# One encoder layer on one core: a fourteenth projection pair as seven half products, and the last gate tiles moved between the branch tiles

## Chip, core and metric

The kernel runs on one core of a Trainium2 chip. The metric is the device time of one execution in microseconds. Before the change three runs took 723.83, 724.24 and 725.03 us, so the median is 724.24 us.

## What is computed

One post-norm encoder layer in float32 on 512 tokens of width 1024, cut here to what matters:

```python
proj = h @ w_in[l]                       # q, k, v of both token mixers, 3840 columns
qa, ka, va, qb, kb, vb = jnp.split(proj, SPLITS, axis=-1)
o_a = windowed_gqa_sink(qa, ka, va, a_sink[l])     # 16 heads
o_b = dilated_mixture(qb, kb, vb)                  # 3 groups of 4 heads, merged
gates = jax.nn.sigmoid(h @ w_gate[l] + b_gate[l])  # 2048 columns
g_a, g_b = jnp.split(gates, N_BRANCH, axis=-1)
mixed = g_a * (o_a @ w_br_a[l]) + g_b * (o_b @ w_br_b[l])
y = mixed @ w_out[l]
h = layer_norm(DN_ALPHA * h + y, ln1_g[l], ln1_b[l])
f = (jax.nn.silu(h @ w_ff_gate[l]) * (h @ w_ff_up[l])) @ w_ff_down[l]
h = layer_norm(DN_ALPHA * h + f, ln2_g[l], ln2_b[l])
```

## The kernel before, in words

**Products.** A float32 product is made of three matmuls on rounded operands: every operand is split into a high part h (a copy rounded to fp32r, line 387 on ACT or 389 on DVE) and a low part l (the rest, a DVE subtraction, line 413 or 558), and h·h + h·l + l·h is added up in PSUM. A projection has units of 128 output columns: U_QA, U_KA, U_VA for mixer A, U_QKB, U_V0, U_VB for mixer B, and 16 gate tiles U_GATE. A unit alone (`feat_x`, lines 537 to 539) is 8 k-steps of three matmuls of 128x512, so 24, from four weight tiles (two h, two l) that `unit` loads and splits.

**Pairs.** `pair_x` (line 608) computes two units together by a seven-product scheme for 2x2 blocks: seven half products of 4 k-steps by three matmuls of 128x256 (lines 659 to 661), so 84 matmuls. It loads five blocks of weights by SP and adds two of them up by accumulating DMAs from POOL (line 401), forms S2 and S4 by two DVE additions (with the letter D: by DMA), splits seven operands, moves four halves out of PSUM by ACT (line 667), and adds the parts on DVE (lines 558 and 682). The combinations of x that it needs are formed once, by `x_forms`. Thirteen pairs are computed so; sixteen units are computed alone.

**Order.** Nothing is written out in queue order by hand. Each operation is given to `Program.op` with its engines, buffers and a priority; `Program.run` (line 207) goes through a model of the five engines in time and lets each free engine take the ready operation with the lowest priority whose buffers fit (`fits`, line 188). What comes out is a fixed instruction order for each engine. A priority is `pr.T` (the PE work given so far, in us) plus an offset: weights -130 (`LOOK`), evacuations -100 (`EV`). Buffers are counted in classes: 85 slots of 128x512, of which `gen`, `ws` (loaded weights) and `whl` (split weights) take shares; four `x4` buffers, which hold the split x until the last product that reads it; eight PSUM banks, of which at most three are of the class `dense` (`BANKS`), which all projections and branches use.

**ORDER** (line 87) is a string of words that `step` (line 1393) takes in turn: `q2` or `k1` a unit alone, `P:` or `D:` a pair, `g` a gate tile, `R` and `r` the rotary turn of the tiles that wait for it (`turn_rows`; r also by DMA), `A0` to `A3` and `B0` to `B3` an attention group, `O` the fetch of a tile of mixer A's output, `V0`, `V12`, `VA` values. `@-31` shifts the priority of that word by -31 us. Before the first word, five units run along each other while x arrives: k0, q0, the first value unit and two gate tiles; k0 and q0 are turned and split right behind that (`k_near`, `q_near`), which empties their PSUM banks.

**Branches.** After the last word come the 16 branch tiles in the order BRANCHES: `branch_a` (8 k-steps, from the fetched output of mixer A) and `branch_b` (2 k-steps), each multiplied by its gate tile (line 1482). `fetch_oa` (line 1365) fetches and splits mixer A's output; the high parts of tiles 4 to 7 (`N_XA` = 4) go into an `x4` buffer, so they wait for one that x has left. Gate tiles 8 to 15 are stored to DRAM and fetched again. Then come the output projection with the first layer norm (`tok_major`), 22 tiles of the channel mixer and the second norm.

Of the kernel before, what the change touches and what calls it, by code (L numbers as in the profile page):

```python
# [15 lines left out]
P = 128  # L16
S = 512
D = 1024
# [13 lines left out]
U_KA = 0  # L32
# [19 lines left out]
BIAS = 0.2  # L52
SPARE, SPARE2 = (4, 12)
ROOMS = {2: dict(whl=16), 3: dict(whl=20, ws=8)}
# [49 lines left out]

BRANCHES = "a0 a1 a2 a3 a4 b0 a5 b1 b2 a6 b3 b4 a7 b5 b6 b7"

# [31 lines left out]
class Program:  # L138


    def __init__(self, limits):
        self.limits = limits
        self.used = {k: 0 for k in limits}
        self.ops = []
        self.writer, self.readers = {}, {}
        self.T = 0.0
        self.spare = SPARE
        self.strict = self.hold = False
        self.rooms = {}

# [56 lines left out]
    def run(self):  # L207
# [27 lines left out]
        while n_left:  # L235
# [13 lines left out]
            while progress:  # L249
                progress = False  # L250
                for e in engines:
# [19 lines left out]
                    for b in o.bufs:  # L271
                        if b.tile is None:
                            if b.keys[0] in self.rooms:
                                b.room = self.rooms[b.keys[0]].popleft()
# [70 lines left out]
def hybrid_layer(ctx: ExitStack, tc: tile.TileContext, wpack, xT, xtok, sink, bgate,  # L345
# [111 lines left out]
    def unit(u):  # L457
        return [half_unit(u, 0), half_unit(u, 1)]
# [33 lines left out]
    for j in range(2):  # L492
        for w, u in (("k", U_KA), ("q", U_QA), ("v", U_VA), *((i, U_GATE + 8 + i) for i in range(N_ALONG))):
            first[w, j] = half_unit_by(u, j, ((0, S),) if j else ALONG_CUTS if w in range(N_ALONG) else CUTS, FIRST[w, j])
# [263 lines left out]

    def in_sbuf(u):

        ps, t = bank("dense"), slot()
        feat_x(ps, unit(u))
        op([(ACT, act(S, True))], lambda e: copy(ACT, halves(t.t), back(ps.t)), reads=[ps], writes=[(t, 1), (t, 2)], prio=EV)
        return t
# [518 lines left out]
    def gate_of(f, t):  # L1283
        gz[f] = t
        op([(ACT, act(S, False, 1))], lambda e: nc.scalar.activation(
            t.t, t.t, AF.Tanh, bias=bg.t[:, f:f + 1], scale=0.5), reads=[(t, 1), (t, 2), bg], writes=[t], prio=EV)
        if f in AWAY:
            put_away(f)
# [6 lines left out]
    def gate(f, ps=None):  # L1295
        if ps is None:
# [6 lines left out]
           reads=[ps, bg], writes=[t], prio=EV)  # L1303
        if f in AWAY:
            put_away(f)
# [6 lines left out]
    def dense_k(u, nt):  # L1312
        ps = bank("dense")
        feat_x(ps, unit(u))
        return k_post(ps, nt) if nt else k_pairs(ps)

    psk, psq, psv = bank("dense"), bank("dense"), bank("dense")
    along = [bank("s") for _ in range(N_ALONG)]
# [11 lines left out]
    for f in range(N_ALONG):  # L1330
        gate(8 + f, ps=along[f])
    ka, qa = {0: k_near(psk, 4)}, {0: q_near(psq, 4, (0, 0))}
    load(mB, maskb, prio=0)
    env = {"gate": N_ALONG, "turn": [], "qs": {}, "ks": {}}

# [29 lines left out]
    def fetch_oa(k):  # L1365
# [8 lines left out]
        return split_of(st, [st], OA_SPLIT, h=Part(xa[k // 4], k % 4) if k >= N_XA else None, by_blocks=True)  # L1374

    def units_of(w):
        i = int(w[1:] or 0)
# [9 lines left out]
        if w[0] == "k":  # L1387
            return U_KA + i, lambda t: ka.update({i: k_post(t, 4)})
        f = (env["gate"] + 8) % 16
        env["gate"] += 1  # L1390
        return U_GATE + f, lambda t: gate_of(f, t)

    def step(w):
        if w == "X":
            x_forms()
        elif w == "L":
            op([(POOL, 0.0)], lambda e: pr.limits.update(ws=N_WS, whl=N_WHL), after=[env["mark"]])
# [31 lines left out]
        elif w[0] in "gG":  # L1429
            for _ in range(int(w[1:] or 1)):  # L1430
                gate((env["gate"] + 8) % 16)
                env["gate"] += 1
        elif w[0] in "QK":
# [16 lines left out]

    for w in ORDER.split():
        w, _, later = w.partition("@")
        pr.T += float(later or 0)
        step(w)
        pr.T -= float(later or 0)
# [5 lines left out]
    op([(POOL, 0.0)], free_all, after=lasts)  # L1461


# [12 lines left out]

    sa.extend(fetch_oa(k) for k in range(len(sa), 8))
    MA = moving(sa)
    sm, sb_ = {}, []

# [13 lines left out]
    def branch_b(f):  # L1494
        if not sb_:
            sb_.extend(split_of(t, [(t, 0), (t, 1)], OB_SPLIT) for t in obT)
        if f % 4 == 0:
            env["wu"] = unit(U_BRB + f // 4)
        MB = moving(sb_)
        ps = bank("dense")  # L1500
        for k in range(2):
            feat_k(ps, env["wu"], k, MB, lambda k: [sb_[k][0].tok, sb_[k][1]], nk=2, col=lambda k: (k, (f % 4) * P))
        mark = gated(8 + f, ps)
# [4 lines left out]

    names = BRANCHES.split()
    marks = []  # L1510
    for n, w in enumerate(names):
        k = 8 + int(w[1])
        if w[0] == "b":
            if k in away:
                fetch_gate(k, [*exps, marks[names.index("b%d" % (k - 11))]] if k > 10 else exps)
        marks.append((branch_a if w[0] == "a" else branch_b)(int(w[1])))
    for w, mark in zip(names, marks):
        env[w] = [mark]


# [594 lines left out]
```

## Time and profile before

| | |
|---|---|
| median of three runs | 724.24 us |
| the profiled execution | 724.82 us |
| its span, first to last instruction | 723.0 us |
| PE busy | 712.5 us (99%), 4947 matmuls |
| DVE busy | 664.4 us (92%) |
| ACT busy | 494.6 us (68%) |
| POOL busy | 173.2 us (24%) |
| DMA | 141.44 MB, mean 196 GB/s |

The profiled execution has 1.8 us outside its span. A matmul's own duration (0.275 us for 128x256, about 0.38 us for 128x512) overlaps the next one; what it costs in a stream is the distance between two starts, which the timeline shows.

### The profile page before, as it was taken

How to read it: one execution, taken by the hardware profiler on the slowest of the kernel's cores; microseconds unless marked ns; L12 is line 12 of the kernel's file. 1: busy time of each engine (PE TensorE's matmuls, PEld its weight loads, DVE VectorE, ACT ScalarE, POOL GpSimd, SP SyncE). 2: the span in 40 equal slices, each digit the busy share in tenths (PEclk: the TensorE clock that was granted, in tenths of full speed). 3: DMA queues.
4: the chain of work that ended last, by engine and by line, in shares of the span. 5: the costliest groups of instructions: out<-in, count | busy, mean ns of one | idle time of the engine just before them, and what ended most of it. 6: DMA issues, size and time to landing. Idle time of an engine off the chain costs nothing.

```text
span 723.0 us, 14810 instructions
## 1 busy us (share of the span) xinstructions
PE 712.5 (99%) x4947; PEld 667.2 (92%) x4947; DVE 664.4 (92%) x1425; ACT 494.6 (68%) x1136; POOL 173.2 (24%) x347
## 2 busy tenths in 40 slices
PE   8999999999999999999999999999999999999996
PEld 6889999998999998988888999999999999999985
DVE  6998999999999989999958998999999999999987
ACT  5768889889878997767625666756567566666821
POOL 0113343322423591550020022121121201212000
PEclk9999999999999999999999999999999999999999
DMA  8978967887568789766690499776897868979402
GB/s 257 294 215 210 235 168 213 227 216 179 137 169 204 187 255 253 219 196 219 199 210 33 110 300 232 177 203 165 238 238 197 223 164 219 253 196 194 106 29 88
DMA packets 81275, 141.44 MB, mean 196 GB/s; under 512 B 11024, under 2 KB 15760, under 8 KB 81200
## 3 DMA queue, kind: packets, MB, share of 16 engines
q1 hardware_dynamic: 63472, 107.07, 46.3%
q0 software_dynamic: 17456, 33.30, 26.6%
q8 instruction: 39, 0.64, 0.4%
q14 instruction: 36, 0.29, 0.1%
q10 hardware_dynamic: 272, 0.13, 0.1%
HBM read 119.69 MB, written 8.39 MB: 177 GB/s over the span
## 4 chain that ended last, share of the span: by engine, by line
PE 90%; DMA 4%; DVE 3%; SPq 2%; ACT 1%; issue 0%; POOL 0%; DVEq 0%; ACTq 0%; POOLq 0%
PE ps L1761 10%; PE ps L1759 10%; PE ps L1760 9%; PE ps L659 5%; PE ps L661 5%; PE ps L660 5%; PE ps L537 4%; PE ps L538 4%; PE ps L539 4%; PE ps L1970 4%; PE ps L1972 4%; PE ps L1971 4%; PE ps L1018 3%; DMA sl<-wpack 3%; PE ps L1549 3%; PE ps L1551 3%
## 5 line engine op out<-in xcount | busy, mean ns | idle before, releaser
L387 ACT ACTIVATE sl<-sl 128x512 fp32r<-128x512 f32 (+3 forms) x457 | 253.8, 588 | 60.7 <-DVE sl L558 43.3
L558 DVE TENSOR_TENSOR sl<-sl,sl 128x512 fp32r<-128x512 f32 (+3 forms) x415 | 245.3, 628 | 6.0 <-ACT sl L387 5.0
L387 ACT ACTIVATE sl<-ps 128x256 f32<-128x256 f32 (+6 forms) x214 | 88.5, 440 | 76.6 <-PE ps L1761 53.0
L401 POOL DMA_DIRECT2D sl<-wpack x70 | 63.0, 931 | 319.1 <-DMA sl<-wpack 92.0
L1760 PE MATMUL ps<-sl,sl 128*128 128x256 f32 x352 | 96.8, 275 | 0.0
L1761 PE MATMUL ps<-sl,sl 128*128 128x256 f32 x352 | 96.8, 275 | 0.0
L1759 PE MATMUL ps<-sl,sl 128*128 128x256 f32 x352 | 96.8, 275 | 0.0
L1759 PE MATMUL ps<-x,sl 128*128 128x256 f32 x264 | 72.6, 275 | 0.0
L1760 PE MATMUL ps<-x,sl 128*128 128x256 f32 x264 | 72.6, 275 | 0.0
L1761 PE MATMUL ps<-x,sl 128*128 128x256 f32 x264 | 72.6, 275 | 0.0
L1759 PEld LDWEIGHTS ps<-sl,sl 128*128 128x128 f32 x352 | 67.6, 192 | 0.1
L1760 PEld LDWEIGHTS ps<-sl,sl 128*128 128x128 f32 x352 | 67.6, 192 | 0.1
L1761 PEld LDWEIGHTS ps<-sl,sl 128*128 128x128 f32 x352 | 67.6, 192 | 0.0
L537 PE MATMUL ps<-x,sl 128*128 128x512 f32 (+1 forms) x161 | 62.1, 386 | 0.7 <-ACT x L387 0.7
L539 PE MATMUL ps<-x,sl 128*128 128x512 f32 (+1 forms) x161 | 60.9, 378 | 0.0
L659 PE MATMUL ps<-sl,sl 128*128 128x256 f32 x208 | 57.8, 278 | 0.9 <-ACT sl L667 0.9
L661 PE MATMUL ps<-sl,sl 128*128 128x256 f32 x208 | 57.3, 276 | 0.0
L660 PE MATMUL ps<-sl,sl 128*128 128x256 f32 x208 | 57.2, 275 | 0.0
L558 DVE TENSOR_TENSOR sl<-sl,ps 128x512 f32<-128x512 f32 (+1 forms) x72 | 47.3, 661 | 9.0 <-PE ps L1972 5.8
L1759 PEld LDWEIGHTS ps<-x,sl 128*128 128x128 f32 x264 | 50.6, 192 | 0.4
L1760 PEld LDWEIGHTS ps<-x,sl 128*128 128x128 f32 x264 | 50.6, 192 | 0.4
L1761 PEld LDWEIGHTS ps<-x,sl 128*128 128x128 f32 x264 | 50.7, 192 | 0.0
(174 smaller groups left out, 2006.6 us busy)
## 6 DMA issues: line engine op xcount, KB each, us to landing
sl<-wpack SPq DMA_DIRECT2D x254, 256.0 KB
sl<-wpack POOLq DMA_DIRECT2D x70, 256.0 KB, 5.5
wf<-wpack SPq DMA_DIRECT2D x51, 256.0 KB
sl<-sl SPq DMA_DIRECT2D x56, 128.0 KB
wf<-wpack POOLq DMA_DIRECT2D x24, 256.0 KB, 5.3
oa<-sl POOLq DMA_DIRECT2D x32, 128.0 KB, 3.6
sl<-sl SPq DMA_DIRECT2D x72, 32.0 KB
gz<-sl SPq DMA_DIRECT2D x8, 256.0 KB
```

The costliest lines, as they stand in the source:

```text
L387: nc.scalar.activation(dst, src, AF.Copy)
L401: op([(POOL, 1.0)], lambda e: nc.gpsimd.dma_start(b.t, src2, accum_op=ALU.add), reads=[b], writes=[b], prio=prio, moves=1.65)
L537: mm(o, a, x0, start=(k == 0 and begins), stop=False, skip_group_check=split)
L538: mm(o, a, x1, start=False, stop=False, skip_group_check=split)
L539: mm(o, b, x0, start=False, stop=(k == nk - 1), skip_group_check=split)
L558: op([(DVE, dve(w))], lambda e: nc.vector.tensor_tensor(dst(), x(), y(), op=o), reads=reads, writes=writes, prio=prio)
L659: mm(o, wh, pairs(bh[k]()), start=(first and k == 0), stop=False, skip_group_check=True)
L660: mm(o, wh, pairs(bl[k]()), start=False, stop=False, skip_group_check=True)
L661: mm(o, wl, pairs(bh[k]()), start=False, stop=(k == 3), skip_group_check=True)
L1759: mm(o, wh, pairs(bh[k]()), start=(first and k == 0), stop=False, skip_group_check=True)
L1760: mm(o, wh, pairs(bl[k]()), start=False, stop=False, skip_group_check=True)
L1761: mm(o, wl, pairs(bh[k]()), start=False, stop=(k == 3), skip_group_check=True)
```

## The change

ORDER, its offsets and some constants are new. The number of words `P:` and `D:` goes from 13 to 14: two gate tiles that were `g` words (tiles 0 and 1) become one pair. k0 and q0 become words of ORDER (`first_of`), so their turning and splitting, and with it the emptying of their PSUM banks, comes at the place and priority of the word. The branch tiles become words of ORDER too; the word `/` runs `late()`, which frees the buffers of the attention and completes the fetches of mixer A's output. The last three gate tiles are 5, as a single unit, and 6 with 7, as a pair; they come behind `/`, just ahead of the branch words. Before, 5 and 6 were a pair, 7 was a single unit, and no branch tile had been given yet. `N_XA` = 8 puts the high parts of all eight tiles of mixer A's output into ordinary slots, none into an `x4` buffer. One turn word (that of Q02 and K02) goes from R to r. A PSUM bank for the accumulators `d` is preferably one that a whole-bank user held last (`room_for`).

```diff
-SPARE, SPARE2 = (4, 12)
+SPARE, SPARE2 = (6, 12)
...
 ORDER = """
-X@-11 VA@-23 q2@-799 q1@-877 P:q3,g@-124 R@-106 D:k1,q4@-31 R@155 P:q5,Q01@-843 A0@-168 D:q6,q7@-47 D:g,g@-34 r@631 P:g,Q00@-22 L@-4 A2@-96
-D:g,K00@-31 A1@-48 R@187 V12@-20 P:g,K01@-67 R@-5 P:Q02,K02@-28 A3@-55 V0@55 R@5 B0@-7 B1@11 O@25 O@35 P:K10,Q10@-39 O@-13 O@-54 K11@-34 R@24
-O@11 P:Q12,Q11@-30 g@28 K12@-12 O@950 g@25 r O@43 P:g,g@-2 B2@-525 O@-304 B3@21 g@-29 P:g,g@-32 g@-8
+X@8 q1@-832 q0@288 P:q3,g@-368 R@-92 D:k1,q4@-30 R@191 P:q5,Q01@-788 q2@-435 k0@40 VA@-106 A0@-163 D:q6,q7@-68 r@1450 D:g,g@-56 P:g,Q00@-1
+L@-33 A1@-75 D:g,K00@-2 A2@-90 V12@-10 R@-8 P:g,K01@-72 R@1 P:Q02,K02@-21 V0@23 r@-570 B0@-107 O@-104 A3@-82 O@-32 P:K10,Q10@-29 B1@-44 O
+K11@-15 O@40 R@696 O@-49 O@42 P:Q12,Q11@-7 P:g,g@13 K12@-34 O@-15 P:g,g@-31 r@-7 B2@-653 O@66 g@2 B3@-265 /@-12 g@21 P:g,g@-51 a0@14 a4@5
+b0@18 a1@-36 b1@7 a5@-3 a6@28 a3@-28 a2@-31 b3@6 b2@20 b4@46 a7@-19 b7@-26 b6@322 b5@-17
 """
-FORMS = -255.0
-VAL = 140.0
-OA_AFTER = (1, 0, 0, 0, 0, 1, 0, 0)
+FORMS = -240.0
+VAL = 80.0
+OA_AFTER = (0, 0, 0, 1, 0, 1, 0, 0)
...
-STORE, OA, OA_SPLIT, OB_SPLIT, N_OA, N_XA = 0.0, -60.0, -140.0, -140.0, 4, 4
+STORE, OA, OA_SPLIT, OB_SPLIT, N_OA, N_XA = 0.0, -60.0, -140.0, -140.0, 4, 8
...
-BRANCHES = "a0 a1 a2 a3 a4 b0 a5 b1 b2 a6 b3 b4 a7 b5 b6 b7"
+GATES = (8, 9, 10, 11, 12, 13, 14, 15, 0, 1, 2, 3, 4, 5, 6, 7)
...
+    def room_for(self, b):
+        free = self.rooms[b.keys[0]]
+        if b.keys[0] != "bank":
+            return free.popleft()
+        room = next((r for r in free if self.whole.get(r)), free[0]) if b.keys[1] == "d" else free[0]
+        free.remove(room)
+        self.whole[room] = b.keys[1] in ("dense", "o", "d", "dff")
+        return room
...
-    ka, qa = {0: k_near(psk, 4)}, {0: q_near(psq, 4, (0, 0))}
+    ka, qa = {}, {}
+    first_of = {"k0": (psk, lambda t, post: ka.update({0: (k_post(t, 4) if post else k_near(t, 4))})),
+                "q0": (psq, lambda t, post: qa.update({0: (q_post(t, 4, (0, 0)) if post else q_near(t, 4, (0, 0)))}))}
...
     def step(w):
         if w == "X":
             x_forms()
+        elif w == "/":
+            late()
+        elif w[0] in "ab":
+            branch(w)
+        elif w in first_of:
+            first_of[w][1](first_of[w][0], False)
...
+    MA, sm, sb_, marks = [], {}, [], []
+
+    def branch(w):
+        f = int(w[1:])
+        if w[0] == "b" and 8 + f in away:
+            fetch_gate(8 + f, [*exps, *env["b%d" % (f - 3)]] if f > 2 else exps)
+        marks.append((branch_a if w[0] == "a" else branch_b)(f))
+        env[w] = [marks[-1]]
+
+    def late():
+        op([(POOL, 0.0)], free_all, after=lasts)
+        sa.extend(fetch_oa(k) for k in range(len(sa), 8))
+        MA.extend(moving(sa))
+        env["late"] = True
```

## Rows read from the trace of the kernel before

**Rows 1.** The page, busy time, share of the span and instructions of an engine.

```profile
PE 712.5 (99%) x4947; PEld 667.2 (92%) x4947; DVE 664.4 (92%) x1425; ACT 494.6 (68%) x1136; POOL 173.2 (24%) x347
```

**Rows 2.** Who waited for whom, PE alone: us in total, times, longest.

```profile
PE ps L473 <- DVE eps L524: 1.2, 1, 1.2
PE ps L659 <- ACT sl L667: 0.9, 1, 0.9
PE ps L537 <- ACT x L387: 0.7, 1, 0.7
PE ps L1018 <- ACT sl L1006: 0.4, 1, 0.4
```

**Rows 3.** Busy time in six stretches: PE, PEld, DVE, ACT, POOL, clock, DMA share, GB/s.

```profile
0.00:44.00 44.00, 41.11 (x209) 34.77 (x210) 36.80 (x82) 28.24 (x58) 4.33 (x9) 1.00 0.91 272
44.00:260.00 216.00, 216.00 (x1631) 206.82 (x1630) 203.17 (x489) 186.19 (x460) 77.07 (x167) 1.00 0.76 195
260.00:300.00 40.00, 39.60 (x242) 35.57 (x241) 36.25 (x96) 29.35 (x76) 16.30 (x42) 1.00 0.94 243
300.00:360.00 60.00, 60.00 (x318) 53.48 (x317) 57.25 (x137) 40.80 (x94) 16.51 (x63) 1.00 0.64 207
360.00:388.00 28.00, 28.00 (x132) 24.51 (x131) 18.09 (x32) 8.76 (x15) 5.25 (x6) 1.00 0.69 169
388.00:723.00 335.00, 327.82 (x2425) 312.07 (x2423) 312.85 (x595) 201.20 (x437) 53.76 (x62) 1.00 0.69 180
```

**Rows 4.** PE's timeline: first and last of 141 single-unit matmuls, then of 48 pair matmuls.

```profile
6.59 0.38 PE L537 MATMUL ps<-x,sl 128*128 128x512 f32 x1
...
36.80 0.38 PE L539 MATMUL ps<-x,sl 128*128 128x512 f32 x1
37.02 0.27 PE L659 MATMUL ps<-x,sl 128*128 128x256 f32 x1
...
42.27 0.28 PE L661 MATMUL ps<-sl,sl 128*128 128x256 f32 x1
```

**Rows 5.** DVE in 40 to 340 us by shape: busy us, mean ns, idle before.

```profile
L558 DVE TENSOR_TENSOR sl<-sl,sl 128x512 fp32r<-128x512 f32 x85 | 57.5, 684 | 4.8 <-ACT sl L387 4.6
L558 DVE TENSOR_TENSOR sl<-sl,ps 128x512 f32<-128x512 f32 x13 | 8.9, 682 | 0.4 <-PE ps L661 0.4
L682 DVE SCALAR_TENSOR_TENSOR sl<-ps,sl 128x256 f32<-128x256 f32 x13 | 5.4, 418 | 0.3 <-PE ps L904 0.2
```

**Rows 6.** ACT in 40 to 340 us by shape.

```profile
L387 ACT ACTIVATE sl<-sl 128x512 fp32r<-128x512 f32 x170 | 101.4, 624 | 10.5 <-DVE sl L558 4.3 <-DMA sl<-oa 2.2 <-PE ps L538 2.2
L667 ACT ACTIVATE sl<-ps 128x256 f32<-128x256 f32 x51 | 19.0, 376 | 4.4 <-PE ps L661 4.3
```

**Rows 7.** The page: POOL's accumulating weight loads, first issues, then issue to landing.

```profile
L401 POOL DMA_DIRECT2D sl<-wpack x70 | 63.0, 931 | 319.1 <-DMA sl<-wpack 92.0
...
sl<-wpack POOLq DMA_DIRECT2D x70, 256.0 KB, 5.5
```

**Rows 8.** PE's timeline around the last matmul on x.

```profile
300.65 0.38 PE L539 MATMUL ps<-x,sl 128*128 128x512 f32 x1
```

**Rows 9.** The chain of waits in 0 to 46 us: start, us, what.

```profile
26.75 7.32 DMA sl<-wpack
...
35.45 0.72 DVE sl L774
...
38.48 0.73 DVE sl L774
...
43.13 0.28 ACT sl L667
```

**Rows 10.** The chain of waits in 255 to 282 us.

```profile
261.01 6.40 DMA sl<-oa
...
278.92 0.41 ACT sl L1006
```

**Rows 11.** Weight loads of PE, by shape: busy us, mean ns.

```profile
L661 PEld LDWEIGHTS ps<-sl,sl 128*128 128x128 f32 x208 | 39.9, 192 | 0.1
```

More of the change, by code (lines that the diff above doesn't have):

```diff
@@ L148, in __init__ @@
         self.strict = self.hold = False
-        self.rooms = {}
+        self.rooms, self.whole = {}, {}
     @staticmethod
@@ L273, in run @@
                             if b.keys[0] in self.rooms:
-                                b.room = self.rooms[b.keys[0]].popleft()
+                                b.room = self.room_for(b)
                                 b.tile = b.make(b.room)
@@ L492, in hybrid_layer @@
     for j in range(2):
-        for w, u in (("k", U_KA), ("q", U_QA), ("v", U_VA), *((i, U_GATE + 8 + i) for i in range(N_ALONG))):
+        for w, u in (("k", U_KA), ("q", U_QA), ("v", U_VA), *((i, U_GATE + GATES[i]) for i in range(N_ALONG))):
             first[w, j] = half_unit_by(u, j, ((0, S),) if j else ALONG_CUTS if w in range(N_ALONG) else CUTS, FIRST[w, j])
@@ L757, in turn_rows, with in_sbuf @@
             op([(POOL, 0.0)], lambda e: None, reads=[(R, "r", 0), (R, "r", 1)], writes=[R], prio=EV)
-    def in_sbuf(u):
-        ps, t = bank("dense"), slot()
-        feat_x(ps, unit(u))
+    def in_sbuf(u, ps=None):
+        t = slot()
+        if ps is None:
+            ps = bank("dense")
+            feat_x(ps, unit(u))
         op([(ACT, act(S, True))], lambda e: copy(ACT, halves(t.t), back(ps.t)), reads=[ps], writes=[(t, 1), (t, 2)], prio=EV)
@@ L1286, in gate_of @@
             t.t, t.t, AF.Tanh, bias=bg.t[:, f:f + 1], scale=0.5), reads=[(t, 1), (t, 2), bg], writes=[t], prio=EV)
-        if f in AWAY:
+        if f in AWAY and not env["late"]:
             put_away(f)
@@ L1303, in gate @@
            reads=[ps, bg], writes=[t], prio=EV)
-        if f in AWAY:
+        if f in AWAY and not env["late"]:
             put_away(f)
@@ L1315, in dense_k @@
         return k_post(ps, nt) if nt else k_pairs(ps)
+    env = {"gate": N_ALONG, "turn": [], "qs": {}, "ks": {}, "late": False}
     psk, psq, psv = bank("dense"), bank("dense"), bank("dense")
@@ L1330, in hybrid_layer @@
     for f in range(N_ALONG):
-        gate(8 + f, ps=along[f])
-    ka, qa = {0: k_near(psk, 4)}, {0: q_near(psq, 4, (0, 0))}
+        gate(GATES[f], ps=along[f])
+    ka, qa = {}, {}
+    first_of = {"k0": (psk, lambda t, post: ka.update({0: (k_post(t, 4) if post else k_near(t, 4))})),
+                "q0": (psq, lambda t, post: qa.update({0: (q_post(t, 4, (0, 0)) if post else q_near(t, 4, (0, 0)))}))}
     load(mB, maskb, prio=0)
-    env = {"gate": N_ALONG, "turn": [], "qs": {}, "ks": {}}
     xa, sa = [None, x4()], []
@@ L1374, in fetch_oa, with next_gate @@
         return split_of(st, [st], OA_SPLIT, h=Part(xa[k // 4], k % 4) if k >= N_XA else None, by_blocks=True)
+    def next_gate():
+        env["gate"] += 1
+        return GATES[env["gate"] - 1]
     def units_of(w):
@@ L1388, in units_of @@
             return U_KA + i, lambda t: ka.update({i: k_post(t, 4)})
-        f = (env["gate"] + 8) % 16
-        env["gate"] += 1
+        f = next_gate()
         return U_GATE + f, lambda t: gate_of(f, t)
@@ L1395, in step @@
             x_forms()
+        elif w == "/":
[4 more added lines that the diff above has]
+            first_of[w][1](first_of[w][0], False)
+        elif w[1:] in first_of:
+            first_of[w[1:]][1](first_of[w[1:]][0], True)
+        elif w[2:] in first_of:
+            ps, f = first_of[w[2:]]
+            env["turn"].append((in_sbuf(None, ps), lambda t, f=f: f(t, True)))
         elif w == "L":
@@ L1430, in step @@
             for _ in range(int(w[1:] or 1)):
-                gate((env["gate"] + 8) % 16)
-                env["gate"] += 1
+                gate(next_gate())
         elif w[0] in "QK":
@@ L1449, in step @@
                 op([(POOL, 0.0)], lambda e: pr.limits.update(ROOMS[hs]), after=list(exps))
[L1451 to L1455, printed above, removed]
     def free_all(e):
@@ L1459, in free_all @@
         pr.spare = SPARE2
-    op([(POOL, 0.0)], free_all, after=lasts)
     def moving(parts):
@@ L1474, in give_room @@
         pr.limits.update(gen=min(pr.limits["gen"] + 1, N_SLOT - N_WS2 - N_WHL))
-    sa.extend(fetch_oa(k) for k in range(len(sa), 8))
-    MA = moving(sa)
-    sm, sb_ = {}, []
+    MA, sm, sb_, marks = [], {}, [], []
[10 more added lines that the diff above has]
+        env["late"] = True
     def gated(f, ps):
@@ L1496, in branch_b @@
             sb_.extend(split_of(t, [(t, 0), (t, 1)], OB_SPLIT) for t in obT)
-        if f % 4 == 0:
-            env["wu"] = unit(U_BRB + f // 4)
+        if ("wu", f // 4) not in env:
+            env["wu", f // 4] = unit(U_BRB + f // 4)
         MB = moving(sb_)
@@ L1507, in branch_b @@
         return mark
[L1509 to L1518, printed above, removed]
+    for w in ORDER.split():
+        w, _, later = w.partition("@")
+        pr.T += float(later or 0)
+        step(w)
+        pr.T -= float(later or 0)
     xt = {(t, j): slot() for t in range(NR) for j in range(2)}
```

2 lines of the change are left out of this document (1 added, 1 removed).

## The prediction

> **What bounds the kernel now.** I read the page's busy shares first. PE stands at 712.5 of 723.0 us and DVE at 664.4 [rows 1], so PE is the bound and DVE is close behind it. A busy share can hide waits, so the next view is the list of who waited for whom, for PE alone: four waits, 3.2 us together [rows 2]. Two of them, 1.2 and 0.7, are of the start, before x has arrived. The other two could be reached by another order: 0.9 us behind an ACT evacuation (line 667) and 0.4 us behind an ACT scaling of probabilities (line 1006). The table by stretches says the same from the other side [rows 3]: PE is idle for 2.89 us up to 44 us, for none up to 260, for 0.40 up to 300, for none up to 388, and for 7.18 after it, in the norms and the stores at the end, which the change doesn't touch. From 44 to 388 us PE misses 0.4 us of 344. An order can't give more than the 1.3 us of the two waits; whatever else is to come must come from fewer or shorter matmuls.
>
> Is a busy PE here also a PE at its pace? The timeline of starts says so [rows 4]. From 6.59 to 36.80 us stand 141 matmuls of 128x512, so 140 distances of 0.2158 us; the 48 of a pair from 37.02 to 42.27 us have 47 distances of 0.1117 us. The granted clock is 1.00, that is 2.4 GHz, in all six stretches [rows 3].
>
> **The fourteenth pair, on PE.** Two single units are 48 matmuls by 0.2158, so 10.36 us. A pair is 84 by 0.1117, so 9.38 us [rows 4]. The difference is 0.98 us less, on the engine that sets the end, in a stretch where it doesn't wait. This is the one certain term.
>
> The Trainium skill weighs against it: TensorE: Matmul & The Clock Gate, section Back-to-back issue gap, gives a stream of weight loads and matmuls about 81 ns per matmul at 128 columns and 131 ns at 512. An estimate on the straight line between them is 98 ns at 256 columns; then two units would take 6.3 us, a pair 8.2 us, and the pair would cost 1.9 us. The distances of rows 4 disagree with both of its ends; they decide.
>
> **The fourteenth pair, on the other engines.** Two units need four splits, a pair seven; so three more copies on ACT (0.624) and three more subtractions on DVE (0.684). The pair also has two additions for S2 and S4 (taken at the same 0.684, the same operation on the same shape), the two additions at its end (0.682 and 0.418) and four moves out of PSUM on ACT (0.376) [rows 5, 6]. DVE: 5 by 0.684 + 1.10 = 4.5 us more. ACT: 3 by 0.624 + 4 by 0.376 = 3.4 us more. The pair is among the words around the second half of mixer B, where DVE has 3.75 us idle of 40 and ACT 10.65 [rows 3]. So I cost it at nothing, but the cover on DVE there is thinner than the work; what hides the rest is that three gate tiles leave that place (next part). Without this the excess of about 0.8 us would stand behind the evacuations that PE waits for.
>
> DMA: seven transfers of 256 KB in place of four, two of them issued by POOL at 0.93 us each, landing after 5.5 us [rows 7]. POOL is busy 16.30 of 40 us there and 16.51 of the next 60, the DMA engines 0.94 and 0.64 of the time [rows 3]. In POOL's queue they stand among the exchanges and the memsets of mixer B; a load that is early by `LOOK` (130 us of priority) doesn't reach PE. Bounds: nothing, or once the 5.5 us of a landing that comes too late; I take nothing, since in the trace 70 such loads left no wait of PE on a transfer [rows 2, 7].
>
> **The last three gate tiles.** PE's work for them is the same, a pair and a single unit, 9.38 + 5.18 = 14.56 us. Before, the last matmul on x starts at 300.65 [rows 8]; now the three stand at the front of the branches. Their DVE work moves too: a pair has 9 by 0.684 + 1.10 = 7.3 us, a single unit 2 by 0.684 = 1.4 us, so 8.6 us leave the stretch up to 300, where the new pair brings 4.5. Balance there: 4.1 us of DVE less. Behind 300 us DVE is idle for 2.75 us up to 360 and for 9.91 up to 388 [rows 3]; the stretch also gets 14.56 us longer by the PE work, so 8.6 fits into 27. The wait of 0.4 us in that stretch is the end of a chain that began with a fetch of mixer A's output (6.40 us) and went on to the ACT scaling [rows 10]; with less on both engines and the fetches in another order I take it as gone. Bounds: 0 to 0.4 us gained. This is also what `N_XA` = 8 is for in terms of buffers: without an `x4` buffer the splits of mixer A's output no longer wait for x, else late gate tiles would hold them. Price: four more slots of 85; PE waits for none [rows 2], so nothing, and up to the 0.4 us of the wait above if a probability tile is kept waiting for its slot.
>
> **k0, q0, the turns and the banks.** Between 27 and 43 us the chain of waits runs over a weight load of 7.32 us, then ACT and DVE, with two rotary shuffles (line 774, 0.72 and 0.73 us) between the splits, up to the evacuation that PE waits for 0.9 us [rows 9, 2]. The new order puts the turning of k0 and q0 later, which takes such shuffles out of this chain; but the load of 7.32 us ahead of it stays, and the first words are still q1 and a pair. So the wait may go (0.9 gained), stay, or grow, since the DMA engines are at 0.91 in that stretch [rows 3] and DVE has no reserve in it but the start. I take it as it is. The turn that goes from R to r takes one shuffle from DVE and gives eight small DMA issues to SP; beside the 0.73 us of a shuffle [rows 9] I cost it at nothing, bounds -0.7 to +0.7. The choice of banks for the accumulators `d` and the new order of branch tiles work behind 360 us, where DVE is idle for 9.9 of 28 us [rows 3]; nothing.
>
> **The sum.** -0.98 (pair) - 0.40 (wait at 279 us) = -1.38 us. Against the profiled execution of 724.82 us that gives 723.44; the median of the runs lies 0.58 lower, at 724.24, so the forecast is 724.24 - 1.38 = 722.86, rounded to 722.9 us. About 0.2%, 1.45 us, is what a measurement of this kernel tells from no change. The forecast lies at that edge.
>
> **Rivals.** *The early wait goes as well.* For it: the shuffles stand in the very chain [rows 9]. Against: the load ahead of them. It gives 724.24 - 0.98 - 1.3 = 721.96.
>
> *The new order has waits of its own that eat the pair's gain.* The order comes from a model of the engines, and the model of the old one missed by 1.3 us of waits [rows 2]. Twice such waits in place of them are worth -0.98 + 1.3 = +0.3, so about 724.5; as little as 0.9 us more leaves 724.2.
>
> *The banks of k0 and q0 make it slower.* Only three banks are `dense`. q0's shift of +288 us keeps its bank until DVE finds nothing more urgent, k0 comes only behind q1, three pairs and q2. A pair needs two banks. With one free, the next product waits for the evacuation of the last: 0.376 for it and 0.624 for a copy ahead of it in ACT's queue [rows 6], 1.0 us each. Place: the first 30 us behind 37 us. For four products that is +4.0, so 724.24 - 1.38 + 4.0 = 726.9. It decides from the second such wait on, which takes the gain away; from the third it is slower than 0.2%. For it: before, two shuffles that read these banks lie at 35.45 and 38.48 us, right where the first pair starts [rows 4, 9]. Against: the modelled order counts banks, and fills such gaps with other units where weights are there.
>
> *Half products are paced by their weight loads.* A weight load lasts 0.192 us [rows 11], longer than the distance of 0.1117. Were they not overlapped, 84 by 0.192 = 16.1 us would replace 10.36: +5.8, 730.0. The thirteen pairs of the trace don't show it [rows 4]. That is the mechanism for which the page named above speaks.
>
> *The change doesn't do what it says* would leave 724.2; fourteen words P and D stand in the new ORDER, so this is left only for the trace to count.
>
> **How the numbers follow.** Forecast 0.36, with its own range 722.3 to 723.4; a good third of it is below 722.8, where the 0.2% begin. Early wait gone 0.27. Gain eaten 0.20. Banks 0.15. Weight loads 0.01, not done 0.01. Faster by over 0.2%: 0.27 + 0.14 = 0.41. Within: 0.22 + 0.20 + 0.01 = 0.43. Slower: 0.15 + 0.01 = 0.16. The range begins at the best case, 721.96, less the 0.6 by which execution and median differ, so 721.4, and reaches to 726.0, which leaves out the upper half of the banks' case and the weight loads, about 0.1, with as much for what I have not thought of.
>
> **What would show it.** Right: lines 659 to 661 count 28 matmuls more each, lines 537 to 539 lose 16 each, and PE's busy time falls by 1.0 us to 711.5; no wait behind line 1006; the last matmul on x some 15 us behind the first branch tile's; DVE fuller between 300 and 360 us. Wrong: PE waits on line 667 or on a transfer between 37 and 70 us, a new wait of PE between 300 and 388 us, or a distance of pair starts other than 0.1117. The forecast is wrong as a whole if PE's waits up to 388 us sum up to much more or less than the 2.9 us that it leaves (2.89 + 0.40 - 0.40).

## Result, and the profile after

The changed kernel takes 726.02 us (median of 19 runs), the kernel before 724.61 in the same comparison: a ratio of 1.002, 95% interval 1.0013 to 1.0027. It is slower by about 0.2%, where 722.9 and a gain were forecast. Measured again on another occasion: 725.92 against 724.39, ratio 1.002 (1.0011 to 1.0029).

One profiled execution of the changed kernel ran at a mean granted clock of 0.655 and took 1062.97 us, so the profile shown here is that of the second measurement (725.43 us, span 723.4, clock 0.998). It is the shortest of its eleven runs, while the profile before (724.82, span 723.0) lies above its median: the two profiles differ by 0.6 us, the medians by 1.5. That has to be kept in mind below.

The page of the changed kernel, busy times and three lines of the pairs' half products (16 of the 28 that each line runs for a pair; `...` marks what is left out):

```profile
PE 712.3 (98%) x4983; PEld 668.3 (92%) x4983; DVE 666.6 (92%) x1425; ACT 499.2 (69%) x1148; POOL 169.7 (23%) x349
...
L669 PE MATMUL ps<-sl,sl 128*128 128x256 f32 x224 | 62.9, 281 | 0.5 <-ACT sl L677 0.5
L671 PE MATMUL ps<-sl,sl 128*128 128x256 f32 x224 | 61.7, 276 | 0.0
L670 PE MATMUL ps<-sl,sl 128*128 128x256 f32 x224 | 61.7, 275 | 0.0
```

It has 36 matmuls more than before [rows 1], as 84 in place of 48 make it. But PE's busy time fell by 0.2 us only, not by 1.0. Who PE waited for:

```profile
PE ps L483 <- DVE eps L534: 1.2, 1, 1.2
PE ps L547 <- ACT x L397: 0.8, 1, 0.8
PE ps L1653 <- DVE sl L1635: 0.6, 1, 0.6
PE ps L669 <- ACT sl L677: 0.5, 2, 0.3
```

Against [rows 2] the wait behind the scaling of probabilities (before: line 1006) is gone, as forecast; one at the first norm's transposes (line 1653, before: 1630) is new. Four stretches, columns as in [rows 3]:

```profile
0.00:44.00 44.00, 41.69 (x215) 35.34 (x216) 37.40 (x84) 29.25 (x59) 4.36 (x9) 1.00 0.92 279
...
260.00:300.00 40.00, 39.77 (x259) 36.29 (x260) 38.09 (x87) 31.99 (x77) 15.87 (x34) 1.00 0.99 241
300.00:360.00 60.00, 60.00 (x325) 53.72 (x325) 54.59 (x141) 40.94 (x100) 15.51 (x68) 1.00 0.66 214
360.00:388.00 28.00, 28.00 (x131) 24.58 (x131) 24.08 (x41) 11.99 (x20) 5.23 (x6) 1.00 0.77 202
```

DVE has 6 us more between 360 and 388 us, not between 300 and 360, where the late gate tiles were expected to load it. Up to 388 us PE is idle for 2.54 us (2.31 + 0.23), close to the 2.9 that the prediction left, so its own sign for being wrong as a whole doesn't show the slowdown.

Busy times hide what is lost, because a matmul's duration is longer than the distance to the next start. So I took all of PE's starts from the timeline, and off each distance its pace ([rows 4]: 0.2158 for 128x512, 0.1117 for 128x256; the other forms by the median distance between two alike). What is left is lost time, small waits too:

| stretch, us | before | after |
|---|---|---|
| 0 to 44 | 2.25 | 1.67 |
| 44 to 240 | 0.57 | 0.53 |
| 240 to 300 | 1.49 | 1.79 |
| 300 to 388 | 0.24 | 0.38 |
| 388 to 420 | 0.57 | 1.28 |
| 420 to the end of PE | -0.04 | -0.04 |
| sum | 5.08 | 5.61 |

Less 0.98 for the pair and 0.53 more lost: the last matmul starts at 715.13 instead of 715.59 us. So PE did end earlier, by 0.46 us. The execution did not, because of what comes behind it. The last rows of DVE, then the issues of the last three stores on SP, first of the kernel before:

```profile
718.50 1.54 DVE L1612 SCALAR_TENSOR_TENSOR sl<-sl,st,sl 128x512 f32<-128x512 f32 x3
719.27 0.33 SPq L2006 DMA_DIRECT2D out<-sl  x1
719.70 0.38 SPq L2006 DMA_DIRECT2D out<-sl  x1
720.17 0.40 SPq L2006 DMA_DIRECT2D out<-sl  x1
```

and the same of the changed kernel:

```profile
718.04 1.54 DVE L1635 SCALAR_TENSOR_TENSOR sl<-sl,st,sl 128x512 f32<-128x512 f32 x3
718.82 0.33 SPq L2029 DMA_DIRECT2D out<-sl  x1
719.25 0.37 SPq L2029 DMA_DIRECT2D out<-sl  x1
720.04 0.33 SPq L2029 DMA_DIRECT2D out<-sl  x1
```

Its DMA queues in the last 4.4 us: packets, MB, share of 16 engines.

```profile
q1 hardware_dynamic: 432, 0.52, 33.3%
q14 instruction: 1, 0.01, 0.5%
```

The same three stores, behind the same DVE work. Before, each issue follows the last within 0.09 us. After, SP stands still from 719.62 to 720.04, 0.42 us (the hole, below), though the third piece is ready at 719.58 (718.04 + 1.54). The last microseconds also hold a packet of the instruction queue, and none before; it starts at 720.87, when SP has already gone on, so it goes with the place and isn't shown to be what SP waits for. From DVE's last end to the span's end it is 723.0 - 720.04 = 2.96 us before and 723.4 - 719.58 = 3.82 after. That is 0.86 us, where the prediction had put nothing.

### The profile page after: what moved, and what is told of

The parts are those of the page before. It is cut to its first block, busy times and chain, and to the rows that moved or that the text cites. A ratio compares the mean times of both kernels' runs of the same rounds, so it can differ in the third digit from the quotient of the medians.

```text
span 1061.0 us, 14969 instructions
## 1 busy us (share of the span) xinstructions
PE 1051.9 (99%) x4983; PEld 885.2 (83%) x4983; DVE 684.8 (65%) x1425; ACT 511.7 (48%) x1148; POOL 160.7 (15%) x349
## 4 chain that ended last, share of the span: by engine, by line
PE 99%; DVE 0%; DVEq 0%; issue 0%
PE ps L1784 10%; PE ps L1783 9%; PE ps L1782 9%; PE ps L671 6%; PE ps L669 6%; PE ps L670 6%; PE ps L548 6%; PE ps L547 6%; PE ps L549 6%; PE ps L1994 4%; PE ps L1993 4%; PE ps L1995 4%; PE ps L1574 3%; PE ps L1573 3%; PE ps L1030 3%; PE ps L1572 3%
## 5 line engine op out<-in xcount | busy, mean ns | idle before, releaser
L568 DVE TENSOR_TENSOR sl<-sl,sl 128x512 fp32r<-128x512 f32 (+3 forms) x424 | 254.4, 631 | 46.8 <-ACT sl L397 44.1
L397 ACT ACTIVATE sl<-ps 128x256 f32<-128x256 f32 (+6 forms) x213 | 91.3, 442 | 278.7 <-PE ps L1784 160.2
L1782 PE MATMUL ps<-sl,sl 128*128 128x256 f32 x352 | 122.9, 349 | 0.0
L1784 PE MATMUL ps<-sl,sl 128*128 128x256 f32 x352 | 122.8, 349 | 0.0
L1783 PE MATMUL ps<-sl,sl 128*128 128x256 f32 x352 | 122.2, 347 | 0.0
L1783 PEld LDWEIGHTS ps<-sl,sl 128*128 128x128 f32 x352 | 92.4, 262 | 0.5 <-issue 0.2
L1782 PEld LDWEIGHTS ps<-sl,sl 128*128 128x128 f32 x352 | 91.9, 261 | 0.4
L1782 PE MATMUL ps<-x,sl 128*128 128x256 f32 x264 | 92.1, 349 | 0.0
L1783 PE MATMUL ps<-x,sl 128*128 128x256 f32 x264 | 91.9, 348 | 0.0
L1784 PE MATMUL ps<-x,sl 128*128 128x256 f32 x264 | 91.8, 348 | 0.0
L1784 PEld LDWEIGHTS ps<-sl,sl 128*128 128x128 f32 x352 | 91.8, 261 | 0.0
L669 PE MATMUL ps<-sl,sl 128*128 128x256 f32 x224 | 79.4, 354 | 0.0
L670 PE MATMUL ps<-sl,sl 128*128 128x256 f32 x224 | 78.0, 348 | 0.0
L671 PE MATMUL ps<-sl,sl 128*128 128x256 f32 x224 | 78.0, 348 | 0.0
L1782 PEld LDWEIGHTS ps<-x,sl 128*128 128x128 f32 x264 | 67.5, 256 | 1.6 <-issue 0.3
L1783 PEld LDWEIGHTS ps<-x,sl 128*128 128x128 f32 x264 | 67.4, 255 | 1.5 <-issue 0.2
L1784 PEld LDWEIGHTS ps<-x,sl 128*128 128x128 f32 x264 | 67.6, 256 | 0.0
L1995 PE MATMUL ps<-sl,sl 128*128 128x512 f32 x126 | 64.7, 514 | 0.0
L1994 PE MATMUL ps<-sl,sl 128*128 128x512 f32 x126 | 64.6, 513 | 0.0
```

The lines of the kernel that those rows point to most:

```text
L397: nc.scalar.activation(dst, src, AF.Copy)
L568: op([(DVE, dve(w))], lambda e: nc.vector.tensor_tensor(dst(), x(), y(), op=o), reads=reads, writes=writes, prio=prio)
L669: mm(o, wh, pairs(bh[k]()), start=(first and k == 0), stop=False, skip_group_check=True)
L670: mm(o, wh, pairs(bl[k]()), start=False, stop=False, skip_group_check=True)
L671: mm(o, wl, pairs(bh[k]()), start=False, stop=(k == 3), skip_group_check=True)
L1782: mm(o, wh, pairs(bh[k]()), start=(first and k == 0), stop=False, skip_group_check=True)
```

## Experiments

Times of the kernel before, run beside each batch: 724.39, 724.47, 724.55 and 724.53 us. Ratios are against it, with the 95% interval.

**The changed kernel again.**

> The changed kernel once more, for a profile at full clock. Theory W (new waits): 14 pairs take 1.0 us of work from PE (busy 711.5), but PE's waits up to 388 us, 3.3 us before, are about 5.7 us now, and the list of waits names them; time about 726.0. Rival C (clock): the waits are as before and the granted clock is lower in some stretch, so that the starts of matmuls there stand further apart. Rival P (the pair isn't worth it): waits as before, PE busy above 712.

725.92 us, as told above. The slowdown is there again; its profile is the one shown.

**One word of ORDER, both ways.** The fourteenth pair taken back in the changed kernel, and put into the kernel before:

```diff
-P:g,g@13
+g@13 g@13
```
```diff
-g@28 K12@-12 O@950 g@25
+P:g,g@28 K12@-12 O@950
```

> The changed kernel with the fourteenth pair taken back: the words g@13 g@13 in place of P:g,g@13, all else as changed. If the pair is worth its 0.98 us and the new waits lie elsewhere, this is 1.0 us slower than the changed kernel, about 727.0. If the pair's own load on DVE, ACT and DMA makes the new waits, it is faster than the changed kernel, 724 to 725.

> The kernel before with the fourteenth pair alone: P:g,g@28 in place of the words g@28 and g@25, the old order else. If the pair's work is hidden beside PE: 724.6 - 1.0 = 723.6. If DVE and ACT have no room for it in the old order, PE gets waits behind lines 667, 1006 or the splits and the time is 724.6 or more.

727.89 us (1.0045, 1.0032 to 1.0058) and 739.96 (1.0215, 1.0196 to 1.0234). Neither is the price of a pair, which is 0.98 us of matmuls. The planner makes a new order of everything behind the word that changes: in the second kernel PE has new waits, the longest 3.1 us in all behind one line of DVE. From such an edit nothing can be read off; an experiment on this kernel has to keep the planned order. The runs below keep PE's order to the last matmul, but for the matmuls left out; only the three with the subtraction of the first norm ordered differ on PE, and those not before 429 us. The changed kernel itself ran in the first batch alone: a difference to its 725.92 carries the 0.16 us by which the batches differ.

**Does PE's relief come through?** Five matmuls of 128x512 (the h·l term for three k of gate tile 0 and two of tile 1 before, for five k of gate tile 4 after) are left out, 1.08 us of PE, as much as the pair saves:

```diff
-            mm(o, a, x1, start=False, stop=False, skip_group_check=split)
+            if not thin:
+                mm(o, a, x1, start=False, stop=False, skip_group_check=split)
```

> The kernel before, with five of the 128x512 matmuls left out (the h times l term of gate tile 0 for three k and of gate tile 1 for two); the order of everything else stays. PE gets 5 x 0.2158 = 1.08 us less, about what the fourteenth pair takes off it. Theory A (PE's own work sets the end, so work taken off it comes through whole, and the changed kernel lost its gain to something that it added): 724.4 - 1.1 = 723.3 us, the span shorter by 1.1, PE's waits as before (3.2 us). Theory B (just behind PE stand other engines, so that PE's relief is taken up in waits further on, whoever relieves it): 724.0 to 724.4, with a new wait of PE of 0.5 to 1 us behind DVE or ACT.

> The changed kernel, with five 128x512 matmuls left out (the h times l term of gate tile 4 for five k), 1.08 us of PE. Theory A (PE's work comes through whole): 725.9 - 1.1 = 724.8 us. Theory B (the relief is taken up by DVE, at the first norm's transposes above all, where PE waited 0.6 us for DVE at 404 us): about 725.7 to 725.9, and that wait grows from 0.6 to 1.5 us or so. The time from the end of the last DVE instruction to the span's end should stay at 3.8 us whichever it is, if it belongs to the instruction streams.

Before: 724.32 us (0.9997, 0.9988 to 1.0006), so not the whole of it. After: 725.32 (1.0015, 1.0007 to 1.0024), 0.6 less than the changed kernel, between the two theories; the interval overlaps the changed kernel's, so the time alone tells little, and the first norm's wait stayed at 0.6 us where theory B had 1.5. PE's waits in the first of them:

```profile
PE ps L474 <- DVE eps L525: 1.2, 1, 1.2
PE ps L1020 <- ACT sl L1008: 1.0, 1, 1.0
PE ps L661 <- ACT sl L669: 0.8, 1, 0.8
```

The wait behind ACT's scaling (line 1008 here, 1006 in [rows 2]) has grown from 0.4 to 1.0 us. Three of the five matmuls left out lay at 274.6 to 276.8 us, just ahead of it: 3 x 0.2158 = 0.65 us, all of it waited away at 278 us. The other chain ends when it ends. So theory B holds for what lies just ahead of a wait, and in the changed kernel likewise a new wait of 0.3 us (line 1223) appears among the matmuls left out at 287 to 291 us. This is also how the 0.4 us of [rows 2] could go without a gain: the list lost it, but the time lost from 260 to 300 us is 1.39 before and 1.53 after (part of the row 240 to 300 above).

**Is DVE's load by the late gates what makes the norm late?** The subtractions for the low parts of the last three gate tiles' weights are left out, copies in their place:

```diff
-nc.vector.tensor_tensor(l.t, src.t, f32(h.t), op=ALU.subtract)
+nc.vector.tensor_copy(l.t, src.t)
```

> The changed kernel, in which the nine subtractions that make the low parts of the last three gate tiles' weights are left out and copies of the same shape stand in their place (0.42 for 0.68 us each, so 2.4 us less DVE work, all of it around the first branch tiles). Theory C (the late gate tiles load DVE so much that the first norm is late): the wait of PE at the first norm's transposes (0.6 us at 404 us) is gone, and the time falls by 0.6 to 0.7, to 725.2. Theory D (the loss is at the end of the program, behind the last compute instruction, and outside the span): the wait may shrink but most of the 1.5 us stays, 725.6 or more, with 3.8 us from the last DVE instruction to the span's end.

725.47 us (1.0016, 1.0007 to 1.0025). PE's waits:

```profile
PE ps L484 <- DVE eps L535: 1.2, 1, 1.2
PE ps L673 <- ACT sl L681: 1.1, 2, 0.9
PE ps L1657 <- DVE sl L1639: 0.6, 1, 0.6
PE ps L675 <- DVE sl L569: 0.3, 1, 0.3
```

With 2.4 us less on DVE the wait at the first norm is what it was, 0.6. Theory C falls: it is not the load. (The time lies between the two theories, and its interval overlaps the changed kernel's; the wait decides.)

**The end of the program.** In the changed kernel and its variants SP stands still behind the 978th instruction of its stream; the compiled program has 996 there, and that of the kernel before has just 978. (The trace records 992 and 974 of them, and the place lies behind the 975th recorded one.) Sixteen, then eighteen tiny loads were put ahead of the first store in the kernel before, and 24 in the changed one (`n` below); their data are read by nobody.

```diff
+            if (t, j) == (0, 0):
+                for i in range(n):
+                    nc.sync.dma_start(padt.t[:, 16 * i:16 * i + 16], bgate)
             nc.sync.dma_start(out[t, :, j * S + c0:j * S + c1], xt[t, j].t[:, c0:c1])
```

> The kernel before, with sixteen tiny loads more on SP ahead of the first store (gate biases into a tile that nobody reads), where SP is idle. They bring SP's instruction stream to about the length that it has in the changed kernel, and compute is not touched. Theory D (where an instruction stream's last fetch falls decides the time behind the last compute instruction): that time grows from 3.0 to between 3.4 and 3.9 us, a packet of the instruction queue appears in it, and the time grows by 0.5 to 0.9, to 724.9 to 725.3. Rival (the tail has another cause, or belongs to a single profiled execution): 724.4, within 0.2 us.

> The kernel before with 18 such tiny loads on SP ahead of the first store, so that its stream is 996 instructions long, and its last stores stand at the same places in it as in the changed kernel. Theory E: a hole of 0.4 us between the last two stores, 3.8 us from the last DVE instruction to the span's end in place of 3.0, and 725.2 to 725.4 us in place of 724.4 (16 loads gave 724.7 and 3.2 us). Rival (the tail belongs to the changed kernel's work): 724.5 to 724.7 as with 16 loads, 3.0 to 3.2 us, no hole.

> The changed kernel with 24 tiny loads more on SP ahead of the first store (gate biases into a tile that nobody reads), where SP is idle; compute is untouched. In the profiles of the changed kernel and of its two variants SP stands still for about 0.4 us between its last stores, each time at the 978th instruction of its stream (996 long; 978 long in the kernel before, so that it ends there), and a packet of the instruction queue follows about 1 us behind. Theory E (SP has to cross into a newly fetched piece of its instructions there, and the changed kernel has this in the middle of the last stores): 24 instructions more ahead put the place among earlier stores, which nobody waits for. The last stores follow each other without a hole, the time from the end of the last DVE instruction to the span's end falls from 3.85 to 3.0 to 3.2 us, and the time from 725.9 to 725.0, by adding work. Rival (the hole is the last store's own, or of the transfers): 3.8 us as before, 725.9.

Sixteen: 724.71 us (1.0006, 0.9997 to 1.0015), short of what theory D gave; 3.21 us from DVE's end to the span's end, no hole between the stores, since the third store is now the last instruction ahead of the place. Eighteen: 725.37 us (1.0012, 1.0003 to 1.0021), 0.82 more than before, 3.83 us, and the hole stands between the second store and the third, as in the changed kernel, though every compute instruction is that of the kernel before:

```profile
719.71 0.33 SPq L2013 DMA_DIRECT2D out<-sl  x1
720.15 0.37 SPq L2013 DMA_DIRECT2D out<-sl  x1
720.95 0.33 SPq L2013 DMA_DIRECT2D out<-sl  x1
```

The changed kernel with 24 more: 725.25 us (1.001, 1.0002 to 1.0019), 0.67 less, by adding work. This interval overlaps the changed kernel's, so here the profile has to decide. The hole is gone:

```profile
720.23 0.33 SPq L2036 DMA_DIRECT2D out<-sl  x1
720.65 0.38 SPq L2036 DMA_DIRECT2D out<-sl  x1
721.13 0.41 SPq L2036 DMA_DIRECT2D out<-sl  x1
```

The hole moves with the stream in both directions, as theory E has it; that SP fetches instructions there is not shown. The size is off: 3.41 us remain to the span's end where 3.0 to 3.2 were expected. The hole accounts for 0.40 of the 0.86: from DVE's end to the last byte stored it is 1.66 us before and 2.06 in the changed kernel. The rest stands between the last byte and the span's end: 1.35 us before, 1.81 in the changed kernel, 1.74 in the kernel before with eighteen loads, 1.77 in the changed kernel with 24.

The traces show what this rest is, though no run was made for it. SP's DMAs report their landing on eight semaphores in turn. At its end SP waits for the eight one after the other, always in the same order, and a wait for one that has long been reached still takes 0.06 us. SP's waits at the end, before and after:

```profile
SPq L2110 <- DMA out<-sl: 1.0, 3, 0.4
SPq L2133 <- DMA out<-sl: 1.6, 1, 1.6
```

Before, SP issues 543 DMAs, the third store is on the eighth semaphore, and SP waits three times, last for the last store. In the changed kernel there are 552, the third store is on the first, SP waits once, and seven waits of 0.06 us follow, 0.43 us. In fourteen profiles, one of each kernel, the stretch from the last byte to the end goes by this place: 1.33 to 1.53 us on the eighth semaphore (four profiles), 1.67 on the third, 1.74 on the second, 1.68 to 1.81 on the first (eight). 24 loads are three full turns of the eight and leave the place as it is; eighteen move it by two. So eighteen loads brought both causes at once, and 24 took only the hole away.

**The first norm.** In the changed kernel ACT and DVE read the same PSUM bank there, ACT for three copies, DVE for one subtraction. DVE's subtraction (line 1667) between 395 and 402 us, what it waited for and who waited for it:

```profile
L1667 DVE TENSOR_TENSOR x<-ps,x x2: 692/692/692, 398.1 to 400.3; 128x512 fp32r<-128x512 f32 x2
its engine sat idle before it (us, times) until:
  ACT sl L397: 1.3, 2
who waited for it (us, times):
  ACT sl L397: 0.8, 1
```

Each engine waits for the other. The order puts the subtraction between ACT's two small copies of one bank; ACT's second copy then has to wait for DVE, and the next token tile's copies queue behind it. The Trainium skill, PSUM — Partial Sum Buffer, section PSUM bank collisions raise a hardware error, gives the rule: accesses of two engines to one bank, two reads too, have to be kept apart by semaphores. The trace shows the two engines kept apart so, ACT for 0.8 us behind DVE's read; what would come without it no run here shows. In the kernel before the subtraction came behind both copies for these two token tiles; for a third, at 405 us, it stood between them there too, and ACT waited 0.76 us. The edit puts it behind them everywhere (and two tiny loads keep SP's stream at 996):

```diff
+            cps.append(copy_by_act(...))
...
                h1l4[j].t[:, :, c], src(), f32(h1h4[j].t[:, :, c]), op=ALU.subtract),
-               reads=[pb, (h1h4[j], t)], writes=[(h1l4[j], t)], prio=NORM)
+               reads=[pb, (h1h4[j], t)], writes=[(h1l4[j], t)], prio=NORM, after=cps)
```

> The changed kernel, in which the first norm's subtraction on DVE (line 1667 of it) is ordered behind both ACT copies that read the same bank, as it came out in the kernel before; two tiny loads keep SP's stream at 996 instructions, so the end of the program stays as it is. In the changed kernel's profile these two engines wait for each other in turn (ACT 0.8 us for the subtraction, DVE 1.3 us for the copies), and PE then waits 0.6 us at 404 us. Theory F (this turn-taking is what makes the first norm late): neither ACT nor PE waits there, PE's work ends 0.6 to 0.7 us earlier, the time is 725.2 to 725.3, and 3.8 us from the last DVE instruction to the end stay. Rival (the stage is late for another reason, such as the later arrival of the first transposes): the wait of PE stays at 0.5 or more, 725.7 to 725.9.

724.62 us (1.0, 0.9991 to 1.0009), 1.3 less than the changed kernel, twice what was expected. The same view, in which nobody waits any more:

```profile
L1669 DVE TENSOR_TENSOR x<-ps,x x2: 674/682/691, 399.0 to 400.2; 128x512 fp32r<-128x512 f32 x2
its engine sat idle before it (us, times) until:
who waited for it (us, times):
```

PE's waits:

```profile
PE ps L484 <- DVE eps L535: 1.2, 1, 1.2
PE ps L670 <- ACT sl L678: 1.1, 2, 0.9
PE ps L548 <- ACT x L398: 0.4, 1, 0.4
PE ps L672 <- DVE sl L569: 0.3, 1, 0.3
```

The wait at the norm's transposes has left the list, and the time lost from 388 to 420 us is 0.03 in place of 1.28, so 1.25 us: also the smaller waits at the earlier transposes are gone, of which the kernel before has some (0.57). Theory F holds; 0.6 in the list of waits was half of the loss. The planner moved a few other things with it (a batch-norm operation at 392 us, two blocks of PE's matmuls behind 429 us), so the subtraction's place was not changed quite alone. From DVE's end it is 3.74 us to the span's end, 0.1 less than in the changed kernel: the two tiny loads put the third store on the third semaphore.

**Both.** The order of the subtraction and the 24 tiny loads.

> The subtraction ordered behind the copies, and 24 tiny loads on SP, both in the changed kernel. If theories E and F both hold and add up: 725.9 - 0.9 - 0.65 = 724.35 us, level with the kernel before (724.45). What is then still missing of the pair's 0.98 us would have to stand in the early wait at 43 us and in small waits up to 340 us. If one of them falls, 725.0 or 725.3; if both, 725.9.

724.07 us (0.9995, 0.9986 to 1.0004): 0.67 + 1.30 = 1.97 expected from the two, 1.85 measured. They add up.

**The early wait.** When a certain weight load lands late (at about 34 us), DVE stands in front of its subtraction with a ready one queued behind. DVE in the changed kernel with relief, in which it landed so:

```profile
34.91 1.29 DVE L570 TENSOR_TENSOR sl<-sl,sl 128x512 fp32r<-128x512 f32 x2 [0.89 <-ACT sl L398]
36.13 0.01 DVE L788 LOAD_MASK_SELECT sl<-ps  x1
36.13 0.73 DVE L788 STREAM_SHUFFLE sl<-ps 128x512 f32<-128x512 f32 x1
```

The edit sets the late one's priority behind the ready one's, alone and with the other two:

```diff
+    pr.ops[214].prio = (-150.0, 214)
     pr.run()
```

> The changed kernel with one subtraction on DVE set behind another: the low part of the weight half whose load lands at about 34 us comes behind a split that is ready at 33 us, as in the kernel before. PE's order is the same. In the changed kernel's runs in which that load came late, DVE stood idle for 0.9 us behind it with the ready split queued after it, and the first pair's matmul waited 0.9 us and more at 43 us; in the run in which it came early there was 0.3 us of wait. Theory G (this queueing is what is still missing): 0.6 us less in late runs, none in early ones, so 725.92 - 0.3 = 725.6, and a wait at 43 us of 0.3 to 0.5 us in the profile. Rival (the relief is taken up by mixer A's end at 260 to 300 us, as when PE was relieved by 1.08 us): the wait at 43 us shrinks and PE loses as much again between 260 and 300 us, 725.8 to 725.9.

> All three in the changed kernel: the subtraction of the first norm behind the copies, 24 tiny loads on SP, and the split set ahead. Theory G: 724.07 - 0.3 = 723.8 us, 0.1% faster than the kernel before (724.5), which is the pair's 0.98 us less the small waits up to 340 us. Rival: 724.1, level with the kernel before within what can be told.

725.66 us (1.0016, 1.0007 to 1.0024) and 723.83 (0.999, 0.9981 to 0.9999). DVE in the second of them:

```profile
34.03 0.69 DVE L569 TENSOR_TENSOR sl<-sl,sl 128x512 fp32r<-128x512 f32 x1
34.92 0.69 DVE L569 TENSOR_TENSOR sl<-sl,sl 128x512 fp32r<-128x512 f32 x1 [0.20 <-ACT sl L398]
...
35.54 0.74 DVE L787 STREAM_SHUFFLE sl<-ps 128x512 f32<-128x512 f32 x1
```

The ready subtraction fills the gap and the shuffle starts 0.59 us earlier (35.54 for 36.13) behind a load that landed alike. PE still waits 0.9 us for the evacuation at 43 us, as it does in the kernel before [rows 2], and theory G's 0.3 to 0.5 us is met only where the load landed early (0.3 in the profile with the split set ahead alone); but with a late load the waiting matmul now starts at 43.57 instead of 44.15 us. The median fell by 0.26 (alone) and 0.24 (with the other two), for 0.3 expected; that is within what can be told, since the intervals are wider. The three together are faster than the kernel before, by 0.7 us, with the interval just clear of 1.

## Why the prediction was wrong

**The pair, -0.98: right on PE.** Its 84 matmuls keep the pace: the median distance between half products is 0.112 us in the kernel before and after. The rival by which weight loads pace them is out. The estimate from the Trainium skill's TensorE: Matmul & The Clock Gate, section Back-to-back issue gap (98 ns per half product, the pair dearer by 1.9 us), doesn't hold against 0.112. With the three edits together, the last matmul starts at 714.53 us, 1.06 earlier than before: -0.98 for the pair, -0.54 in the first norm (0.03 against 0.57), +0.38 from 240 to 388 us, +0.08 ahead of 240. The end is still 0.46 longer (3.42 us against 2.96), the seven waits, so 0.6 of it are left in the span and 0.70 between the medians.

**The wait at 279 us, -0.40: gone from the list, not gained.** The stretch loses no less than before (1.53 against 1.39 us from 260 to 300), and the run with PE relieved shows why: what PE is spared just ahead of a wait comes back as wait. A wait's length is no price; PE's time ahead of it and the chain that ends it are two different things.

**"Behind 360 us, where DVE is idle for 9.9 of 28 us; nothing": the first step that failed.** The first norm lost 0.71 us more than before (1.28 against 0.57). The reason is no lack of DVE time, as the run with less DVE work shows, but the order of two engines at one bank. A share of idle time says how much work fits, and not in which order a chain of handovers goes. The prediction had a rival for it, waits of the new order's own, with 724.2 to 724.5 and 0.20, and it named a wait between 300 and 388 us as what would prove it wrong; the wait came at 404. The rival that came nearest in time, the banks of k0 and q0 (726.9), did so by luck: four waits of 1.0 us don't stand there, and PE lost 2.20 us ahead of 240 us in the profile, against 2.82 before.

**"Gives eight small DMA issues to SP; ... I cost it at nothing", and "the stores at the end, which the change doesn't touch": the second step that failed.** The stores' instructions are the same, but their place in SP's stream and their semaphores are not, and that cost 0.86 us in the profile, 0.82 in the kernel before with eighteen loads more. Eighteen is the number of instructions that the change adds to SP's stream: nine DMA issues and nine that wait for a semaphore. One issue is the pair's, five weight loads in place of four; eight are the turn word that went from R to r (SP's issues of 16 KB, before and after):

```profile
sl<-sl SPq DMA_DIRECT2D x28, 16.0 KB
sl<-sl SPq DMA_DIRECT2D x36, 16.0 KB
```

The prediction had looked at these as transfers and as issue time, with bounds of -0.7 to +0.7 for the turn; that they move the last stores, at the other end of the program, it did not see.

**The early wait: taken as it is, about right.** It differs from run to run, 0.3 to 0.9 us with the landing of one load, which the new order makes worse by 0.6 us when it is late; 0.26 in the median.

**The sum.** Between the two profiles shown: -0.98 (pair) + 0.53 (lost time) + 0.86 (end) + 0.2 (outside the span) = +0.6, as measured between them. The medians differ by 1.5, because PE's loss ahead of 388 us varies: 4.1 to 5.0 us in three profiles of the old order (before, sixteen and eighteen loads), 4.6 on average; 4.4 to 5.8 in five of the changed one (again, copies, 24 loads, subtraction ordered, both), 5.0 on average; nearly all of this difference lies ahead of 60 us. From 240 to 388 us alone the old order loses 1.5 to 3.0 us, so the 0.42 between the two profiles there is no finding. With the averages, an estimate: -0.98 + 0.47 (ahead of 388) + 0.71 (first norm) + 0.86 (end) + 0.16 (outside the span, 1.95 on average instead of 1.79) = +1.2, for 1.5 measured. What the other 0.3 are, and why the time outside the span is longer, stays open. The edits close it from the other side: the subtraction's order gives back 1.30 in the median, the 24 loads another 0.55, the split set ahead 0.24, together 2.09, which turns 1.5 slower into 0.7 faster.

## What to carry to other kernels

With PE at 99%, as here, half of the loss lay where nobody computes: follow the span to its last byte, and count what an edit adds to each engine's instruction stream, and to its number of DMA issues, not only to its work. Read lost time from the distances between starts, and ask of each wait which chain ends it: work taken away just ahead of a wait is not gained. Where two engines read one PSUM bank, order all reads of the one ahead of those of the other.

## What the runs showed of the hardware

SP stands still for 0.40 to 0.43 us, where it otherwise goes on within 0.09, at one place of its instruction stream, behind 978 instructions: between the second and the third of the last stores with 996 instructions (the changed kernel, with relief, with the subtraction ordered, the kernel before with 18 loads more), one store earlier with 997 (the runs with copies and with the split set ahead). A packet of the instruction queue starts 1.0 to 1.3 us behind the place, also where it lies at the very end. Which buffer this is no view shows.

A wait of SP for a semaphore that has long been reached takes 0.06 us, and where the last store isn't on the last of the eight semaphores, up to seven of them stand behind its landing.
